# Feed-forward norm of a hybrid decoder: undivided halves of x written during attention's output product, the root applied to gate and up, new states one step at a time

## Chip, cores and metric

The kernel runs on one core of one Trainium2 chip (the chip is trn2). The metric is device time in microseconds of that core from start to end of one launch; three runs give a median. The engines are TensorE (PE in the profile, with PEld for its weight loads), VectorE (DVE), ScalarE (ACT), GpSimd (POOL) and SyncE (SP), whose queue starts the DMAs.

## What is computed

The reference is one inference step of two layers on 1024 prompt tokens and 8 x 4 sample tokens (1056 columns in all), model width 1024, feed-forward width 2816. Of a layer, cut to what matters here:

```python
    x = x + jnp.concatenate([o_attn, y_ssm], axis=-1) @ p['w_out']   # o_attn 512 wide, y_ssm 1024 wide
    hn = rms_norm(x, p['norm_ffn'])                                   # x * rsqrt(mean(x*x) + EPS) * g
    g, up = jnp.split(hn @ p['w_gate_up'], [D_FF], axis=-1)
    x = x + (jax.nn.silu(g) * up) @ p['w_down']
```

Besides x the layer returns window keys and values, the convolution's last rows, and the new recurrent state of every sample, `h * exp(sum) + sum_t B_t (x) xdt_t`, for 8 samples and 16 heads of 64 x 128. These sample states are the "new states" below.

## The kernel before

Everything lies transposed: x is eight tiles `big` of 128 rows (model width) by 1056 tokens. Tokens are taken in three column groups `t` of TW = 352. Products are made in three passes (`mm3`, lines 258 to 265): each float32 operand is divided into a rounded part and a remainder (`split`, line 226, for activations: ACT casts, DVE or POOL subtracts; `load_next`, line 237, for weights: ACT casts at line 243, POOL subtracts at line 244), and PE adds hi x hi, hi x lo and lo x hi into one PSUM bank. A product of eight 128-row blocks is 24 matmuls of 352 columns, one of four blocks is 12. These products use three rotating banks `g`; all else uses five banks `p`. So the result of a product has to be read out of its bank before the third product after it starts.

The order of work on each engine is in program order as far as dependencies allow, but the framework's scheduler weaves it; engines then run their queues strictly in order. `Flow` (line 81) holds side work as generators: every `tick` (one per product) steps the queue of side work once, runs what `later` put off by a number of ticks, and, for the `slow` queue, makes two steps placed behind the last instruction named as `anchor`.

The stages around the change, per layer:

- Attention (lines 1030 to 1098) is side work during `one_ssm` (line 1189), the output product of the state-space rows: product m is three 24-matmul groups. L1066 and L1067 are the score matmuls, L1017 the scores with mask on DVE, L1024 the exponential on ACT, L1027 the division on DVE, L1082 the transposes on PE (copied out at L1083), L1090 the products with v (copied out at L1093). Products m = 0 to 5 run with attention; then `flow.need` finishes attention, its result is split (L228, L232), product 6 follows.
- Attention's output product (loop from line 1210): eight m, three t, 12 matmuls each; m = 7 takes the state-space rows of m = 7 along. After each, DVE adds it to x (L1217), ACT squares (L318) and DVE adds up the squares in `acc` (L319).
- The norm (`norm_end`, line 321): four one-column matmuls sum the squares over the rows (L292), DVE takes the root by three Newton steps on 88 x 4 numbers (`rsqrt`, lines 275 to 281), PE spreads it over all rows (L300), and for each of eight blocks DVE multiplies x by gain and root (L325), ACT casts (L228), POOL or DVE subtracts (L232).
- The feed-forward block: `hpair` (line 1224) makes gate (part 0) and up (part 1) for 22 blocks f; ACT reads the gate from its bank with SiLU (L1234), DVE multiplies by up (L1236) and the result is split for the down product. The first f goes t by t, gate and up; the others gate for three t, then up. Blocks of 5, 5, 4, 4, 4 f are followed by `accumulate` (line 334), the down product, whose results DVE adds to x at L343.
- The new states (`new_states`, line 1240): 16 tiles, two buffers `F`; each is loaded with its B rows (L1245, L1246), gets four steps of one scaling (L1249) and four multiply-adds (L1251) on DVE, and is written back (L1253). They start 45 ticks into the feed-forward block, two steps a tick.

Of the kernel before, what the change touches and what calls it, by code (L numbers as in the profile page):

```python
# [10 lines left out]
F32 = mybir.dt.float32  # L11
# [6 lines left out]
P = 128  # L18
# [62 lines left out]
class Flow:  # L81


    def __init__(self, tc):
        self.tc, self.anchor = tc, None
        self.queue, self.slow, self.soon, self.open = deque(), deque(), [], set()

    def push(self, name, gen, after=0):
# [8 lines left out]

    def push_slow(self, name, gen):
        self.open.add(name)
        self.slow.append((name, gen))  # L100
# [12 lines left out]
    def tick(self, n=1):  # L113
        due = []
        for e in self.soon:
            e[0] -= 1
            if e[0] < 0:
                due.append(e)
        for e in due:
            self.soon.remove(e)  # L120
            e[1]()
        for _ in range(n + (len(self.queue) > 1)):
            self.step()
        if self.slow and self.anchor:

            with self.tc.issue_after(self.anchor.ins):
                for _ in range(2):
                    self.step(self.slow)
# [20 lines left out]
def body(ctx: ExitStack, tc, A, outs):  # L149
# [170 lines left out]

    def norm_end(x, gcol, u, t, acc):
        r = on_all(rstd_of(acc, D))
        for k in range(KD):
            s = mk("nu", [P, TW], bufs=3)
            V.scalar_tensor_tensor(s, x[k][:, tsl(t)], gcol(k), r, op0=ALU.mult, op1=ALU.mult)  # L325
            split(u[0][t][:, k, :], u[1][t][:, k, :], s, G if k % 4 else V)
# [10 lines left out]
    def accumulate(x, name, nk, xs, norm=None, after=None):  # L337
# [17 lines left out]
        if late:  # L355
            ws = [weights(name + (m,)) for m in (4, 6)]
            for t in range(NT):
                for m in range(4, 8):
                    one(m, t, ws[m // 2 - 2], m % 2 * P)
                if norm:  # L360
                    gcol, u, acc = norm
                    flow.later(lambda t=t: norm_end(x, gcol, u, t, acc[t]))
                else:
                    after(t)
# [10 lines left out]
    for l in range(L):  # L375
# [21 lines left out]
        for part in IN_ORDER:  # L397
# [5 lines left out]
            wlist.append(((l, part), a))  # L403
        for m in list(range(7)) + [("a", m) for m in range(7)] + [7, ("a", 7)]:
            if isinstance(m, int):
# [95 lines left out]
    for l in range(L):  # L501
# [699 lines left out]
        for t in range(NT):  # L1201
            for i in range(4):
                split(ohl[i][0][:, tsl(t)], ohl[i][1][:, tsl(t)], qT[i][:, tsl(t)])
        one_ssm(6, weights((l, "ssm", 6)))

        u = act_tiles()
        acc = accs()
        for m in range(8):
            ws = [weights((l, "ssm", 7))] if m == 7 else []
            ws.append(weights((l, "attn", m)))  # L1210
            for t in range(NT):
                pt = gbank()
                if m == 7:
                    mm3(pt[:, 0:TW], ws[0], 0, P, halves(mix)(t), 8, stop=False)
                mm3(pt[:, 0:TW], ws[-1], 0, P, rows(ohl)(t), 4, start=(m < 7))
                d = x[m][:, tsl(t)]
                flow.anchor = V.tensor_tensor(d, pt[:, 0:TW], d, op=ALU.add)  # L1217
                norm_sq(m, d, acc[t])
                if m == 7:
                    flow.later(lambda t=t, l=l: norm_end(x, lambda k: g_ffn(l, k), u, t, acc[t]), 0)  # L1220
                flow.tick()


        def hpair(f, hh, hl, swap):
# [4 lines left out]
            for part, t in order:  # L1229
                pt = gbank()  # L1230
                mm3(pt[:, 0:TW], ws[part], 0, P, halves(u)(t), KD)
                if part == 0:
                    sg[t] = mk("R", [P, 380], bufs=3)[:, 0:TW]
                    SC.activation(sg[t], pt[:, 0:TW], AF.Silu)  # L1234
                else:
# [44 lines left out]

        flow.later(lambda g=new_states(): flow.push_slow("st", g), after=45)
        flow.open.add("st")
# [47 lines left out]
```

## Time and profile before

| | us |
|---|---|
| three runs, median (lowest to highest) | 2939.91 (2937.18 to 2940.93) |
| the profiled execution | 2939.68 |
| its span, first to last instruction | 2937.9 |
| PE busy, share of the span | 2862.7, 97% |
| DVE, ACT, POOL busy | 1501.2, 1023.3, 998.3 |
| chain that ended last | PE 78%, DVE 12%, DMA 5%, ACT 3% |

Layer 0 takes about the first half of the span, with attention's end near 611 to 638 us, attention's output product to 692 us, then the feed-forward block; the same places of layer 1 lie near 2063, 2090 and 2144 us. A PE record lasts about 0.32 us while the next starts 0.16 us after it, so two overlap: busy time on PE hides losses, and the count of records in a window is what shows them. "PEclk" is the granted share of TensorE's full clock (1.00 is the upper of its two levels, 2.4 GHz; at 1.2 GHz it is half).

### The profile page before, as it was taken

Reading aid. Unit: us, or ns where it says so; the run is one execution under the profiler, and the core shown is the slowest. Engines: PE = TensorE matmul, PEld = TensorE weight load, DVE = VectorE, ACT = ScalarE, POOL = GpSimd, SP = SyncE. Lnnn points to the kernel's source line nnn. Section 1 sums busy time; section 2 is a strip of 40 time slices with the busy share of each in tenths; the row PEclk is TensorE's granted clock in tenths of the full one; section 3 lists DMA queues with packets and bytes.
Section 4 is the critical chain, followed back from the end, with each engine's and each line's share of the span. In section 5 each row is a group of like instructions: output and inputs, shape, how many; then the busy total and the mean of one; then the engine's idle time right before and its main releaser. Section 6 shows DMA issues by size and latency. Waiting matters only on the chain.

```text
span 2937.9 us, 46615 instructions
## 1 busy us (share of the span) xinstructions
PE 2862.7 (97%) x18580; PEld 2746.3 (93%) x18580; DVE 1501.2 (51%) x3689; ACT 1023.3 (35%) x2043; POOL 998.3 (34%) x880
## 2 busy tenths in 40 slices
PE   8999999999999999999989999999999999999999
PEld 6999999879999999999978999998899999999999
DVE  7977747666149411121488677567641683121212
ACT  5564437553211111111256635465431111111111
POOL 5343327434223322222143423355342232222221
PEclk9999999999999999999999999999999999999999
DMA  5231223011125211111222312230111342111112
GB/s 186 74 89 58 78 57 112 17 29 55 46 70 152 69 54 37 58 37 54 73 79 76 88 52 78 56 104 19 40 51 40 98 136 60 52 45 43 54 37 81
DMA packets 307808, 197.76 MB, mean 67 GB/s; under 512 B 27742, under 2 KB 287110, under 8 KB 307560
## 3 DMA queue, kind: packets, MB, share of 16 engines
q1 hardware_dynamic: 307560, 194.79, 22.4%
q8 instruction: 146, 2.39, 0.3%
q14 instruction: 70, 0.57, 0.1%
q10 hardware_dynamic: 32, 0.01, 0.0%
HBM read 171.49 MB, written 25.30 MB: 67 GB/s over the span
## 4 chain that ended last, share of the span: by engine, by line
PE 78%; DVE 12%; DMA 5%; ACT 3%; issue 1%; POOL 1%; SPq 0%; DVEq 0%; POOLq 0%; ACTq 0%
PE g L263 23%; PE g L265 22%; PE g L264 22%; DVE F L1251 2%; DVE big L612 2%; PE p L1090 1%; DMA F<-acd 1%; DVE F L681 1%; ACT nu L897 1%; DMA out_dram<-F 1%; PE p L708 1%; PE p L719 1%; PE p L1082 1%; PE p L692 1%; PE p L778 1%
## 5 line engine op out<-in xcount | busy, mean ns | idle before, releaser
L263 PE MATMUL g<-ahi,whi 128*128 128x352 f32 (+1 forms) x3792 | 1244.3, 329 | 11.4 <-DVE R L1236 6.9
L264 PE MATMUL g<-alo,whi 128*128 128x352 f32 (+1 forms) x3792 | 1230.9, 325 | 7.2 <-DVE alo L232 4.1
L265 PE MATMUL g<-ahi,w 128*128 128x352 f32 (+1 forms) x3792 | 1233.2, 325 | 0.0
L244 POOL TENSOR_TENSOR w<-w,whi 128x1024 fp32r<-128x1024 f32 (+3 forms) x250 | 514.9, 2060 | 1178.5 <-ACT whi L243 937.5
L263 PEld LDWEIGHTS g<-ahi,whi 128*128 128x128 f32 (+1 forms) x3792 | 715.2, 189 | 29.7 <-DVE R L1236 9.2
L264 PEld LDWEIGHTS g<-alo,whi 128*128 128x128 f32 (+1 forms) x3792 | 717.8, 189 | 15.7 <-DVE alo L232 5.5
L265 PEld LDWEIGHTS g<-ahi,w 128*128 128x128 f32 (+1 forms) x3792 | 716.4, 189 | 8.8 <-issue 6.1
L243 ACT CAST whi<-w 128x1024 fp32r<-128x1024 f32 (+3 forms) x250 | 226.1, 904 | 717.0 <-PE g L264 654.9
L1236 DVE TENSOR_TENSOR R<-R,g 128x352 f32<-128x352 f32 x132 | 68.6, 519 | 650.4 <-PE g L265 650.4
L263 PE MATMUL g<-A,whi 128*128 128x352 f32 x1104 | 356.4, 324 | 0.2
L265 PE MATMUL g<-A,w 128*128 128x352 f32 x1104 | 356.0, 322 | 0.0
L264 PE MATMUL g<-F,whi 128*128 128x352 f32 x960 | 310.9, 324 | 0.8 <-DVE F L232 0.6
L343 DVE TENSOR_TENSOR big<-g,big 128x352 f32<-128x352 f32 x240 | 125.7, 524 | 323.3 <-PE g L265 323.2
L263 PEld LDWEIGHTS g<-A,whi 128*128 128x128 f32 x1104 | 207.4, 188 | 0.8 <-DVE big L343 0.7
L265 PEld LDWEIGHTS g<-A,w 128*128 128x128 f32 x1104 | 207.3, 188 | 0.0
L264 PEld LDWEIGHTS g<-F,whi 128*128 128x128 f32 x960 | 180.4, 188 | 5.6 <-DVE F L232 2.4
L228 ACT CAST A<-R 128x352 fp32r<-128x352 f32 x132 | 64.2, 486 | 348.4 <-DVE R L1236 347.7
L1251 DVE SCALAR_TENSOR_TENSOR F<-F,xdds 128x128 f32<-128x128 f32 x512 | 164.2, 388 | 3.2 <-DMA F<-cbd 3.1
L612 DVE SCALAR_TENSOR_TENSOR big<-R,vc,big 128x352 f32<-128x352 f32 (+2 forms) x240 | 140.3, 609 | 15.4 <-ACT big L610 14.3
L685 POOL TENSOR_TENSOR F<-F,A 128x1024 f32<-128x1024 f32 x32 | 87.8, 2744 | 145.3 <-ACT F L684 128.1
L1234 ACT ACTIVATE R<-g 128x352 f32<-128x352 f32 x132 | 60.6, 462 | 207.7 <-PE g L265 207.7
L232 POOL TENSOR_TENSOR F<-R,A 128x352 fp32r<-128x352 f32 x54 | 58.7, 1087 | 143.6 <-ACT A L228 143.6
(332 smaller groups left out, 3337.0 us busy)
## 6 DMA issues: line engine op xcount, KB each, us to landing
w<-in_w_gate_up_dram SPq DMA_DIRECT2D x88, 512.0 KB
w<-in_w_in_dram SPq DMA_DIRECT2D x44, 512.0 KB
F<-acd SPq DMA_DIRECT2D x32, 512.0 KB
out_dram<-F SPq DMA_DIRECT2D x42, 256.0 KB
w<-in_w_down_dram SPq DMA_DIRECT2D x32, 320.0 KB
w<-in_w_down_dram SPq DMA_DIRECT2D x40, 256.0 KB
xd<-big SPq DMA_DIRECT2D x16, 528.0 KB
big<-xd SPq DMA_DIRECT2D x16, 528.0 KB
```

What stands on the lines that cost most here:

```text
L228: SC.copy(hi, src)
L243: SC.copy(hi, raw)
L244: G.tensor_tensor(lo, raw, hi.bitcast(F32), op=ALU.subtract)
L263: TE.matmul(out, lhsT=hi[:, k, c], rhs=xh, start=(start and k == 0), stop=False)
L264: TE.matmul(out, lhsT=hi[:, k, c], rhs=xl, start=False, stop=False)
L265: TE.matmul(out, lhsT=lo[:, k, c], rhs=xh, start=False, stop=(stop and k == nk - 1))
L343: flow.anchor = V.tensor_tensor(d, pt[:, 0:TW], d, op=ALU.add)
L612: flow.anchor = V.scalar_tensor_tensor(d, r(w), c_w(l, w, m), d, op0=ALU.mult, op1=ALU.add)
L685: G.tensor_tensor(bc, bc, ct[:, sl].unsqueeze(1).to_broadcast([P, 2, 512]), op=ALU.mult)
L1234: SC.activation(sg[t], pt[:, 0:TW], AF.Silu)
L1236: flow.anchor = V.tensor_tensor(sg[t], sg[t], pt[:, 0:TW], op=ALU.mult)
L1251: V.scalar_tensor_tensor(st[:, jj, :], bb[:, t, :], xdds[:, j, b * 4 + t:b * 4 + t + 1], st[:, jj, :], op0=ALU.mult, op1=ALU.add)
```

## The change

1. Product m = 7 of the state-space rows is made right after product 6, by itself; attention's product m = 7 is then 12 matmuls as the others.
2. During attention's output product, each new block of x is at once written as its two halves times the gain, without the root: ACT multiplies and rounds (hi), DVE multiplies and subtracts (lo). The squares are added up by POOL and not by DVE.
3. `norm_end`'s 24 multiplications, casts and subtractions are dropped for this norm. The root is taken after m = 7, spread over all rows when the first gate product of that t is done, and copied to `rinv` (ACT). Gate is multiplied by it before SiLU and after it (the second stands for up's root). That is DVE, ACT, DVE where ACT stood alone, for all 22 f.
4. For the norm between the layers the root is taken two ticks ahead of the rest of `norm_end`.
5. `push_slow` takes a pace; new states go one step a tick.

```diff
-                for _ in range(2):
+                for _ in range(self.pace):
                     self.step(self.slow)
...
-    def norm_end(x, gcol, u, t, acc):
-        r = on_all(rstd_of(acc, D))
+    def norm_end(x, gcol, u, t, root):
+        r = on_all(root)
...
-                    flow.later(lambda t=t: norm_end(x, gcol, u, t, acc[t]))
+
+                    def root(t=t):
+                        y = rstd_of(acc[t], D)
+                        flow.later(lambda: norm_end(x, gcol, u, t, y))
+                    flow.later(root)
...
-        for m in list(range(7)) + [("a", m) for m in range(7)] + [7, ("a", 7)]:
+        for m in list(range(8)) + [("a", m) for m in range(8)]:
...
-        one_ssm(6, weights((l, "ssm", 6)))
+        for m in (6, 7):
+            one_ssm(m, weights((l, "ssm", m)))
...
+        r01, r2 = mk("sc", [P, 2, TW]), mk("xs3", [P, TW])
+        rinv = [r01[:, 0], r01[:, 1], r2]
...
+        def root(t):
+            roots[t] = rstd_of(acc[t], D)
+
         for m in range(8):
-            ws = [weights((l, "ssm", 7))] if m == 7 else []
-            ws.append(weights((l, "attn", m)))
+            w = weights((l, "attn", m))
             for t in range(NT):
                 pt = gbank()
-                if m == 7:
-                    mm3(pt[:, 0:TW], ws[0], 0, P, halves(mix)(t), 8, stop=False)
-                mm3(pt[:, 0:TW], ws[-1], 0, P, rows(ohl)(t), 4, start=(m < 7))
+                mm3(pt[:, 0:TW], w, 0, P, rows(ohl)(t), 4)
                 d = x[m][:, tsl(t)]
                 flow.anchor = V.tensor_tensor(d, pt[:, 0:TW], d, op=ALU.add)
-                norm_sq(m, d, acc[t])
+                hi = u[0][t][:, m, :]
+                SC.activation(hi, d, AF.Copy, scale=g_ffn(l, m))
+                V.scalar_tensor_tensor(u[1][t][:, m, :], d, g_ffn(l, m), hi.bitcast(F32), op0=ALU.mult, op1=ALU.subtract)
+                if m == 0:
+                    SC.activation(acc[t], d, AF.Square)
+                else:
+                    sq = mk("nsq", [P, TW], bufs=2)
+                    SC.activation(sq, d, AF.Square)
+                    G.tensor_tensor(acc[t], acc[t], sq, op=ALU.add)
                 if m == 7:
-                    flow.later(lambda t=t, l=l: norm_end(x, lambda k: g_ffn(l, k), u, t, acc[t]), 0)
+                    flow.later(lambda t=t: root(t))
                 flow.tick()
...
                 if part == 0:
+                    if t in roots:
+                        SC.copy(rinv[t], on_all(roots.pop(t)))
                     sg[t] = mk("R", [P, 380], bufs=3)[:, 0:TW]
-                    SC.activation(sg[t], pt[:, 0:TW], AF.Silu)
+                    V.tensor_tensor(sg[t], pt[:, 0:TW], rinv[t], op=ALU.mult)
+                    SC.activation(sg[t], sg[t], AF.Silu)
+                    V.tensor_tensor(sg[t], sg[t], rinv[t], op=ALU.mult)
...
-        flow.later(lambda g=new_states(): flow.push_slow("st", g), after=45)
+        flow.later(lambda g=new_states(): flow.push_slow("st", g, 1), after=45)
```

Three places show how instructions move. In the rows `g` is a product's bank, `p` another bank, `ahi`/`alo` the halves of an activation, `whi`/`w` those of a weight; the line numbers of the change are those of its own file.

The first is PE at the end of attention in layer 0 (L1082/L1088 transpose the weights of attention, L1090/L1096 multiply by v, L1066/L1072 make scores). Before:

```order
L265 MATMUL g_6739<-ahi_4784,w_6269 128x352
L1082 MATMUL p_6465<-cst,F_813_6212 128x128 x4
L1082 MATMUL p_6471<-cst,F_813_6212 128x128 x4
L1082 MATMUL p_6478<-cst,F_818_6239 128x128 x4
L1082 MATMUL p_6484<-cst,F_818_6239 128x128 x4
L1090 MATMUL p_6515<-F_847_6464,A_562_4232 64x512
L1090 MATMUL p_6515<-F_850_6477,A_562_4232 64x512
L1066 MATMUL p_6527<-xs_671_5087,sc_6490 128x256
```

With the change:

```order
L267 MATMUL g_6738<-ahi_4784,w_6269 128x352
L1088 MATMUL p_6465<-cst,F_813_6212 128x128 x4
L265 MATMUL g_6771<-ahi_4782,whi_6682 128x352
L266 MATMUL g_6771<-alo_4785,whi_6682 128x352
L267 MATMUL g_6771<-ahi_4782,w_6683 128x352
...
L265 MATMUL g_6771<-ahi_4782,whi_6682 128x352
L1088 MATMUL p_6471<-cst,F_813_6212 128x128 x4
L266 MATMUL g_6771<-alo_4785,whi_6682 128x352
L267 MATMUL g_6771<-ahi_4782,w_6683 128x352
L1088 MATMUL p_6478<-cst,F_818_6239 128x128 x4
L1088 MATMUL p_6484<-cst,F_818_6239 128x128 x4
```

The 72 matmuls of the state-space product m = 7 now stand among attention's last transposes, scores and products, all of them ahead of the last eight products with v but one; before, nothing of another kind stood there until attention's own output product began.

The second is PE at the step from attention's output product to the first gate product (L292/L294 sum squares, L300/L302 spread the root). Before:

```order
L265 MATMUL g_7382<-A_885_6654,w_7177 128x352
L300 MATMUL p_7247<-cst,r4y_7233 128x88 x4
L292 MATMUL p_7325<-cst,R_6772 88x1 x4
L263 MATMUL g_7494<-ahi_6765,whi_7182 128x352
L263 MATMUL g_7521<-ahi_6765,whi_7484 128x352
L264 MATMUL g_7494<-alo_6768,whi_7182 128x352
```

With the change:

```order
L267 MATMUL g_7419<-ahi_6849,w_7305 128x352
L294 MATMUL p_7346<-cst,R_6855 88x1 x4
L294 MATMUL p_7385<-cst,R_6856 88x1 x4
L265 MATMUL g_7419<-ahi_6849,whi_7304 128x352
...
L265 MATMUL g_7502<-ahi_6850,whi_7304 128x352
L302 MATMUL p_7444<-cst,r4y_7352 128x88 x4
L294 MATMUL p_7454<-cst,R_6857 88x1 x4
L266 MATMUL g_7502<-alo_6853,whi_7304 128x352
```

The sums of squares of t = 0 and t = 1 stand behind the first 18 matmuls of gate (g_7419), and the first root is spread behind gate, up (g_7474) and the first two matmuls of the next gate; before, root and halves stood ahead of the first gate matmul.

The third is DVE between two blocks f while new states are made (L1249/L1275 and L1251/L1277 are a state's steps, L1236/L1262 multiplies by up). Before:

```order
L1236 TENSOR_TENSOR R_9308<-R_9308,g_9400 128x352
L1249 TENSOR_SCALAR F_1190_9429<-F_1190_9429,eends_519 128x128 x4
L1251 SCALAR_TENSOR_TENSOR F_1190_9429<-F_1190_9429,xdds_518 128x128 x3
L232 TENSOR_TENSOR F_1172_9192<-R_9308,A_1171_9191 128x352
L1251 SCALAR_TENSOR_TENSOR F_1190_9429<-F_1190_9429,xdds_518 128x128 x10
L1249 TENSOR_SCALAR F_1203_9521<-F_1203_9521,eends_519 128x128 x3
...
L1251 SCALAR_TENSOR_TENSOR F_1203_9521<-F_1203_9521,xdds_518 128x128 x16
L1236 TENSOR_TENSOR R_9481<-R_9481,g_9571 128x352
```

With the change:

```order
L1262 TENSOR_TENSOR R_9210<-R_9210,g_9285 128x352
L1275 TENSOR_SCALAR F_1166_9314<-F_1166_9314,eends_519 128x128 x4
L1277 SCALAR_TENSOR_TENSOR F_1166_9314<-F_1166_9314,xdds_518 128x128 x3
L234 TENSOR_TENSOR F_1149_9100<-R_9210,A_1148_9099 128x352
L1277 SCALAR_TENSOR_TENSOR F_1166_9314<-F_1166_9314,xdds_518 128x128 x7
L1258 TENSOR_TENSOR R_9361<-g_9336,sc_6858 128x352
L1277 SCALAR_TENSOR_TENSOR F_1166_9314<-F_1166_9314,xdds_518 128x128 x6
L1260 TENSOR_TENSOR R_9361<-R_9361,sc_6858 128x352
```

Before, 40 state instructions stand between one reading of a bank by DVE and the next, with the change 14; the reading is now that of gate (L1258), three products earlier than that of up.

## Rows read from the trace of the kernel before

**Rows 1.** The page, part 1: busy us, share, instructions of each engine.
```profile
PE 2862.7 (97%) x18580; PEld 2746.3 (93%) x18580; DVE 1501.2 (51%) x3689; ACT 1023.3 (35%) x2043; POOL 998.3 (34%) x880
```

**Rows 2.** PE by stretch: window, length, busy (records), PEclk, DMA share, GB/s.
```profile
611.10:625.80 14.70, 12.13 (x67) 0.88 0.12 36
625.80:638.40 12.60, 12.14 (x53) 1.00 0.00 1
638.40:692.60 54.20, 54.20 (x342) 1.00 0.18 52
692.60:730.00 37.40, 32.35 (x188) 0.91 0.19 54
730.00:800.00 70.00, 70.00 (x442) 1.00 0.19 55
840.00:1000.00 160.00, 156.97 (x971) 0.99 0.41 118
1100.00:1300.00 200.00, 200.00 (x1248) 1.00 0.15 43
2062.90:2077.20 14.30, 11.28 (x66) 1.00 0.07 19
...
2144.20:2182.00 37.80, 33.87 (x190) 0.86 0.18 54
2300.00:2460.00 160.00, 155.83 (x952) 0.99 0.41 116
```

**Rows 3.** PE's timeline near attention's end: start, us, instruction, count.
```profile
603.22 1.94 PE L1090 MATMUL p<-F,A 128*64 128x512 f32 x8
...
611.23 1.91 PE L1082 MATMUL p<-cst,F 128*128 128x128 f32 x16
```

**Rows 4.** PE by line, 611.1 to 625.8: busy us, mean ns, idle before and releasers.
```profile
L1090 PE MATMUL p<-F,A 128*64 128x512 f32 x13 | 5.2, 764 | 2.4 <-ACT F L1083 2.4
L1082 PE MATMUL p<-cst,F 128*128 128x128 f32 x36 | 4.6, 278 | 0.1
```

**Rows 5.** PE by line, 692.6 to 730: busy, mean ns, idle before and releasers.
```profile
L264 PE MATMUL g<-alo,whi 128*128 128x352 f32 x53 | 18.7, 356 | 2.6 <-POOL alo L232 1.8 <-DVE alo L232 0.8
...
L300 PE MATMUL p<-cst,r4y 88*128 88x88 f32 x12 | 1.5, 245 | 1.6 <-DVE r4y L281 1.6
```

**Rows 6.** The timeline of all engines in attention's output product.
```profile
650.25 0.52 DVE L1217 TENSOR_TENSOR big<-g,big 128x352 f32<-128x352 f32 x1
650.87 0.50 ACT L318 ACTIVATE nsq<-big 128x352 f32<-128x352 f32 x1 [1.09 <-DVE big L1217]
651.40 0.53 DVE L319 TENSOR_TENSOR R<-R,nsq 128x352 f32<-128x352 f32 x1 [0.62 <-ACT nsq L318]
...
651.84 0.52 DVE L1217 TENSOR_TENSOR big<-g,big 128x352 f32<-128x352 f32 x1
652.40 1.29 POOL L244 TENSOR_TENSOR w<-w,whi 128x512 fp32r<-128x512 f32 x1 [4.04 <-ACT whi L243]
...
652.98 1.10 DVE L319 TENSOR_TENSOR R<-R,nsq 128x352 f32<-128x352 f32 x1 [0.62 <-ACT nsq L318]
```

**Rows 7.** DVE by line, 640 to 692.
```profile
L319 DVE TENSOR_TENSOR R<-R,nsq 128x352 f32<-128x352 f32 x20 | 16.6, 831 | 12.2 <-ACT nsq L318 12.2
```

**Rows 8.** POOL by line, 640 to 692.
```profile
L244 POOL TENSOR_TENSOR w<-w,whi 128x512 fp32r<-128x512 f32 (+1 forms) x7 | 11.3, 1611 | 27.4 <-ACT whi L243 27.4
```

**Rows 9.** POOL by line and shape, whole span: an addition of 352 columns.
```profile
L801 POOL TENSOR_TENSOR A<-A,nu 128x352 f32<-128x352 f32 x24 | 24.0, 1002 | 27.6 <-ACT nu L800 27.6
```

**Rows 10.** ACT by line and shape, whole span: scaling by a column.
```profile
L936 ACT ACTIVATE A<-g,vc 128x352 f32<-128x352 f32 x24 | 13.3, 553 | 0.4
```

**Rows 11.** DVE by line, 840 to 1000, while new states are made.
```profile
L1251 DVE SCALAR_TENSOR_TENSOR F<-F,xdds 128x128 f32<-128x128 f32 x256 | 80.7, 381 | 0.7 <-DMA F<-cbd 0.6
...
L1236 DVE TENSOR_TENSOR R<-R,g 128x352 f32<-128x352 f32 x15 | 7.7, 514 | 16.5 <-PE g L265 16.5
```

**Rows 12.** PE's timeline while new states are made.
```profile
911.69 0.43 PE L263 MATMUL g<-ahi,whi 128*128 128x352 f32 x1 [2.02 <-DVE R L1236]
```

More of the change, by code (lines that the diff above doesn't have):

```diff
@@ L86, in __init__ @@
         self.queue, self.slow, self.soon, self.open = deque(), deque(), [], set()
+        self.pace = 2
     def push(self, name, gen, after=0):
@@ L96, in later, with push_slow @@
         self.soon.append([after, f])
-    def push_slow(self, name, gen):
+    def push_slow(self, name, gen, pace=2):
+        self.pace = pace
         self.open.add(name)
@@ L1203, in body @@
                 split(ohl[i][0][:, tsl(t)], ohl[i][1][:, tsl(t)], qT[i][:, tsl(t)])
-        one_ssm(6, weights((l, "ssm", 6)))
+        for m in (6, 7):
+            one_ssm(m, weights((l, "ssm", m)))
         u = act_tiles()
         acc = accs()
+        r01, r2 = mk("sc", [P, 2, TW]), mk("xs3", [P, TW])
+        rinv = [r01[:, 0], r01[:, 1], r2]
+        roots = {}
+        def root(t):
+            roots[t] = rstd_of(acc[t], D)
         for m in range(8):
-            ws = [weights((l, "ssm", 7))] if m == 7 else []
-            ws.append(weights((l, "attn", m)))
+            w = weights((l, "attn", m))
             for t in range(NT):
                 pt = gbank()
-                if m == 7:
-                    mm3(pt[:, 0:TW], ws[0], 0, P, halves(mix)(t), 8, stop=False)
-                mm3(pt[:, 0:TW], ws[-1], 0, P, rows(ohl)(t), 4, start=(m < 7))
+                mm3(pt[:, 0:TW], w, 0, P, rows(ohl)(t), 4)
                 d = x[m][:, tsl(t)]
                 flow.anchor = V.tensor_tensor(d, pt[:, 0:TW], d, op=ALU.add)
-                norm_sq(m, d, acc[t])
+                hi = u[0][t][:, m, :]
[7 more added lines that the diff above has]
+                    G.tensor_tensor(acc[t], acc[t], sq, op=ALU.add)
                 if m == 7:
-                    flow.later(lambda t=t, l=l: norm_end(x, lambda k: g_ffn(l, k), u, t, acc[t]), 0)
+                    flow.later(lambda t=t: root(t))
                 flow.tick()
```

## Prediction

> **What bounds the kernel now.** I read the page's engine shares first: PE is busy 97% of the span, DVE 51%, ACT 35%, POOL 34% [rows 1]. So the end is set by PE, and a gain can only come from stretches in which PE does less than it could. Busy time hides those, because records overlap; therefore I next read the windows with their counts of records. In the down products 1248 matmuls of 352 columns take 200 us, 0.160 us each; in gate and up 442 take 70 us, 0.158 us each [rows 2]. That pitch is what PE can do: 3.8 us for a product of 24 matmuls, 1.9 us for one of 12. Held against it, each layer has three places where PE falls behind, and one where it does not:
>
> - Attention's end, 611.1 to 638.4 us: few records, and the granted clock is 0.88 in the first part, 1.00 in the second [rows 2].
> - Attention's output product, 638.4 to 692.6 us: 342 x 0.158 = 54.0 of 54.2 us. Nothing is lost.
> - The norm up to the first gate products, 692.6 to 730 us: 188 records in 37.4 us, clock 0.91 [rows 2].
> - The new states, 840 to 1000 us: 971 records in 160 us where 998 would fit [rows 2].
>
> Then I read the groups by line for what ended PE's waits in each [rows 4, 5], and the timelines for who holds whom [rows 6, 12]. The profiled execution took 2939.68 us (2937.9 of span and 1.8 around it), 0.2 below the median of the runs, so the sum below is set against 2939.7.
>
> **A, attention's end.** PE's prices without waits: a transpose 1.91/16 = 0.12 us, a product with v 1.94/8 = 0.243 [rows 3]; scores of 256 columns by their columns, 0.158 x 256/352 = 0.115. The first part holds 36 transposes and 13 products with v [rows 4], 16 scores and 2 others: 4.3 + 3.2 + 1.8 + 0.3 = 9.6 us of work in 14.7, so 5.1 are lost, the lower clock's share among them; in layer 1, with 66 records in 14.3, 4.7. The second part (53 records: 13 transposes, 12 products with v, 28 of 352 columns) holds 1.6 + 2.9 + 4.4 = 8.9 in 12.6 us, so 3.7 are lost. PE waits there for attention's chain on ACT, as for the copies of transposes (L1083) [rows 4], with nothing else in its queue. The change lays the 72 matmuls of product m = 7, 72 x 0.158 = 11.4 us, among just these rows. That is more than is lost, but they stand ahead of the last products with v, so the last copies and the splits of attention's result keep their distance to PE. I take the first part's loss and a little of the second: **5.5 a layer, 11 in both**. Bounds: 3.0 a layer if only the idle time that the busy columns admit comes back (14.70 - 12.13 and 12.60 - 12.14 [rows 2]), 8.6 if all does.
>
> **N, from the norm to gate.** Of the 188 records 28 are small: 37.4 - 160 x 0.158 - 28 x 0.12 = 8.7 us lost; in layer 1 (190 records, 24 of them small, clock 0.86) 37.8 - 166 x 0.158 - 24 x 0.12 = 8.7. The waits are for the halves from POOL, DVE and ACT and for the root [rows 5]. After the change the halves exist already when gate begins, and the root is needed only when gate is read out of its bank. PE has three banks, so three products, 11.5 us, pass before that reading holds it. What may remain are the sums of squares of t = 1, which stand behind 18 gate matmuls (2.8 us) and need POOL's last addition (1.0 us [rows 9], behind an ACT square of 0.50 [rows 6]), and the spreading of the root (L302). Today the root costs PE 1.6 [rows 5]; I leave 1.2 a layer, bounds 0 and 3.5.
>
> **U, the new load in attention's output product.** Today DVE adds (0.52) and sums squares (0.53), ACT squares [rows 6]. Now a product runs DVE add 0.52, ACT hi 0.55 (scaling by a column [rows 10]), DVE lo 0.53, so with a hand-over of some 0.04 about 1.64 us, during which DVE's queue stands still for ACT, against 1.90 us of PE. Over 24 products that leaves 24 x 0.26 = 6.2 us, and two products in spare banks are another 3.8: 10.0 us of cushion. Against it stands what POOL does to DVE: a DVE addition that runs beside a POOL subtraction took 1.10 us in place of 0.53 and ended 0.39 after POOL's end [rows 6]; over the stage 20 additions took 16.6 us, 6.0 more than 20 x 0.53, with POOL busy for 11.3 [rows 7, 8]. The change gives POOL 21 additions of 1.0 [rows 9]: 32.3 us busy. In proportion DVE would be held 6.0 x 32.3/11.3 = 17.2 us, 7.2 beyond the cushion: that is the upper bound, the lower is 0, because POOL's addition is released by the square, which ACT makes after hi, at the time when lo already runs. I take 1.5 a layer.
>
> The Trainium skill (SBUF — State Buffer, "SBUF: two separate sides") states as a rule that a VectorE operation with two SBUF inputs and a GpSimd operation lock one port pair against each other for a whole instruction; the held addition agrees. Its page GPSIMD Engine Reference, "Engine selection", speaks against the change: elementwise additions belong on VectorE, GpSimd being about twice as slow; 1.00 beside 0.53 agrees. By that rule alone the first rival below would be the forecast.
>
> N and U together: 8.7 - 1.2 - 1.5 = **6.0 a layer, 12 in both**; bounds from 8.7 - 3.5 - 7.2 = -2.0 to 8.7 a layer.
>
> **S, the new states.** 160 - 971 x 0.1603 = 4.3 us are lost in layer 0, 160 - 952 x 0.1603 = 7.4 in layer 1: 11.7. A state instruction takes 0.381 us on DVE [rows 11]; two steps a tick are ten, 3.8 us, as long as a product, and DVE has 0.51 for reading up [rows 11] and the splits besides. So its queue runs late by up to 40 state instructions (15.4 us) between two readings, and PE waits for a bank, 2.02 us at 911.69 [rows 12]. One step a tick is 1.9 us; with gate's two multiplications (0.52 and 0.53) 3.0 of 3.8. In the next block's down products of 15 matmuls (2.4 us) DVE has 1.9 + 0.52: some 24 of them run late by 0.05, 1.2 us in all, which the banks hold. Before the reading of gate 14 state instructions, 5.4 us, stand ahead, against two products of cushion, 7.6. I leave 0.8 a layer: **gain 10**, bounds 0 and 11.7.
>
> **Edits at nothing.** 66 gates a layer get two DVE multiplications, 66 x 1.05 = 69 us of DVE each, spread over 66 gate ticks of 3.8 us; DVE has half its time free [rows 1], and the cover is the three banks: without them each gate would cost PE the read, 0.5. SiLU from SBUF and three copies are ACT's, with 65% free. The earlier root of the norm between the layers leaves PE's order as it was. On SP, ACT and POOL, the loads, casts and subtractions of m = 7's state-space weights move ahead of attention's weights; their number is the same, and PE takes them in that order too. The first state load of layer 1 goes out later but stands far ahead of its use.
>
> **Sum.** 11 + 12 + 10 = 33 of 2939.7: **2907 us**. All terms at the top, 17 + 17.4 + 11.7 = 46, give 2893.6; all at the bottom, 6 - 4 + 0 = 2, give 2938.
>
> **The rivals.** (1) *DVE and POOL do share in proportion*, so U costs 7.2 a layer, 11.4 more than I took: 2918. For it the lengthened additions [rows 6, 7]; against it the order of hi, lo and square. 0.20. The Trainium skill's lock (SBUF — State Buffer, "SBUF: two separate sides") is this mechanism. (2) *The wait for new states stays*: one step a tick stretches them over twice as many products, into the short down products, and readings queue behind them there; S gains nothing: 2917. For it, the 2.42 against 2.4; against, the cushion. 0.10. (3) *The fill gives nothing*, that is, the change does not do what it does on paper: attention's end is set by the chain on ACT and DVE, the 72 matmuls delay the products with v as much as they cover: 2918. Against it, PE waits there for short copies only [rows 4]. 0.06. (4) *Slower: each lo and each addition hold one another in turn.* A product's DVE chain is then 1.64 + 1.0 (a whole POOL addition) + 0.47 (the part of a weight subtraction) = 3.1 against 1.90 of PE: 24 x 1.2 = 29, less the 3.8 of the banks, 25 a layer, 23.5 more than I took: 2907 + 47 = 2954. It decides the sign from a chain of 2.8 us: 0.91 late a product, 24 x 0.91 - 3.8 = 18 a layer, 16.5 more than I took, in both layers the sum's 33. Against it: POOL would have to be released just ahead of each lo. 0.04. My forecast has 0.60.
>
> **How the numbers follow.** A measurement of this kernel tells about 0.2%, 5.9 us, from no change. The forecast and the first three rivals give 2907 to 2918 and lie below 2934; two of them together with a weak A (3.0 in place of 5.5) give some 2929 to 2935. So faster 0.89, within 0.2% 0.07, slower 0.04. The range begins at 2892, all at the top, and ends at 2929, which takes in two rivals at once; the slower case and the worst sums are left out.
>
> **What the profile after should show.** A: attention's end with 72 more records and no longer in proportion, clock near 1.00. U: 12 matmuls still every 1.90 us, lo at 0.53 to 0.8 in the mean; a mean over 1.2 with PE waiting for DVE's x would speak for rivals 1 or 4. N: the first 160 gate and up matmuls in some 26.5 us, waits for the root at L294 or L302 under 1.5. S: over 990 records in 160 us, no wait of 2 us for DVE's reading; DVE with over 100 us more busy time. I am wrong if attention's output product takes over 57 us, or if the waits in the states' stretch move to gate's reading.

## The result and the profile after

The changed kernel takes 2904.5 us (median of four runs, 2902.42 to 2910.45), the kernel before 2939.49 (four runs, 2937.18 to 2940.93): the ratio is 0.9883, with a 95% interval of 0.9872 to 0.9895, or some 35 us. The forecast was 2907 with a range from 2892 to 2929. The profiled execution took 2903.36, with a span of 2901.4, against 2939.68 and 2937.9.

The page of the changed kernel, its first part (busy us, share, instructions), against [rows 1]:

```profile
PE 2842.4 (98%) x18580; PEld 2737.2 (94%) x18580; DVE 1718.6 (59%) x3905; ACT 1031.5 (36%) x2049; POOL 980.9 (34%) x886
```

PE has the same number of matmuls and DVE 217 us more work, in a span that is 36.5 us shorter. PE by stretch, the columns as in [rows 2]:

```profile
612.00:624.00 12.00, 12.00 (x80) 1.00 0.08 22
624.00:636.00 12.00, 12.00 (x80) 1.00 0.01 1
636.00:645.00 9.00, 8.88 (x44) 1.00 0.10 29
...
660.00:675.00 15.00, 15.00 (x95) 1.00 0.24 69
...
829.00:989.00 160.00, 160.00 (x1006) 1.00 0.32 92
...
2285.00:2445.00 160.00, 160.00 (x1006) 1.00 0.34 101
```

Attention's end (612 to 645) is now dense at full clock; attention's output product still makes a matmul every 0.158 us (95 in 15); and the 160 us with new states hold 1006 matmuls where there were 971 and 952. PE's waits from 686 to 735 us (what waited for what: us, times, longest), where the kernel before had 5.0 us of them (4.2 stand in [rows 5]), and then the same place of layer 1, 2118 to 2170 us:

```profile
PE g L265 <- DVE big L1231: 0.3, 1, 0.3
```

```profile
PE g L265 <- DVE big L1231: 0.9, 1, 0.9
```

These are PE's first gate matmuls, which wait until DVE has read x's block out of the bank that they are to use.

To see where the time went I take four marks at which both kernels have done the same work, and ask how far the changed one is ahead there: the reading of the last product of m = 5 (L1194, now L1200), the start of the last matmul of attention's output product, the sixth multiplication by up (L1236, now L1262), and the last addition of the down product (L343, now L345).

| mark | layer 0: before, after, ahead | layer 1: before, after, ahead |
|---|---|---|
| m = 5 read | 593.43, 596.89, -3.5 | 2045.23, 2031.13, 14.1 |
| attention's output made | 692.52, 688.88, 3.6 | 2143.97, 2123.40, 20.6 |
| sixth up | 750.95, 739.01, 11.9 | 2202.40, 2174.10, 28.3 |
| last down | 1475.71, 1458.59, 17.1 | 2930.52, 2894.05, 36.5 |

The differences between the rows are the terms of the forecast. Attention's end and its output product (A and U): 7.1 and 6.5, in all 13.6. The norm to gate (N): 8.3 and 7.7, in all 16.0. The new states (S): 5.2 and 8.2, in all 13.4. Together 43.0; and the stretches up to m = 5, which the forecast did not mention, took 3.5 and 3.0 longer. 43.0 - 6.5 = 36.5, the whole difference of the spans. All this compares one profile of each kernel; what that is worth is told behind the table below.

### The profile page after: what moved, and what is told of

It reads as the page before. It is cut to its first block, busy times and chain, and to the rows that moved or that the text cites. A ratio compares the mean times of both kernels' runs of the same rounds, so it can differ in the third digit from the quotient of the medians.

```text
span 2901.4 us, 46904 instructions
## 1 busy us (share of the span) xinstructions
PE 2842.4 (98%) x18580; PEld 2737.2 (94%) x18580; DVE 1718.6 (59%) x3905; ACT 1031.5 (36%) x2049; POOL 980.9 (34%) x886
## 3 DMA queue, kind: packets, MB, share of 16 engines
q8 instruction: 146, 2.39, 0.3%
## 4 chain that ended last, share of the span: by engine, by line
PE 81%; DVE 10%; ACT 5%; DMA 2%; issue 1%; POOL 1%; SPq 0%; DVEq 0%; ACTq 0%; POOLq 0%
PE g L265 24%; PE g L267 23%; PE g L266 23%; DVE big L618 2%; ACT nu L903 2%; DVE F L687 2%; PE p L1096 1%; DMA F<-acd 1%; PE p L714 1%; DVE alo L1234 1%; PE p L1088 1%; PE p L698 1%; DVE F L692 1%; PE p L725 1%; PE p L784 1%
## 5 line engine op out<-in xcount | busy, mean ns | idle before, releaser
L345 DVE TENSOR_TENSOR big<-g,big 128x352 f32<-128x352 f32 x240 | 125.4, 522 | 233.6 <-PE g L267 232.9
L1277 DVE SCALAR_TENSOR_TENSOR F<-F,xdds 128x128 f32<-128x128 f32 x512 | 203.9, 424 | 9.6
L1262 DVE TENSOR_TENSOR R<-R,g 128x352 f32<-128x352 f32 x132 | 68.9, 522 | 216.7 <-PE g L267 215.9
L1259 ACT ACTIVATE R<-R 128x352 f32<-128x352 f32 x132 | 65.6, 497 | 297.6 <-DVE R L1258 297.4
L1258 DVE TENSOR_TENSOR R<-g,sc 128x352 f32<-128x352 f32 x88 | 45.9, 522 | 127.4 <-PE g L267 124.8
```

Source lines behind the costliest of these rows:

```text
L1259: SC.activation(sg[t], sg[t], AF.Silu)
L1262: flow.anchor = V.tensor_tensor(sg[t], sg[t], pt[:, 0:TW], op=ALU.mult)
L1277: V.scalar_tensor_tensor(st[:, jj, :], bb[:, t, :], xdds[:, j, b * 4 + t:b * 4 + t + 1], st[:, jj, :], op0=ALU.mult, op1=ALU.add)
```

## The experiments

All were measured beside runs of the kernel before on the same chip. The table splits each profiled execution by the same marks: by how much it is ahead of the kernel before's profiled execution (both layers added) in the stretches up to m = 5 ("front"), from there to the sixth up ("middle": A, U and N), and from there to the last down product ("states": S).

| kernel | median us (lowest to highest) | ratio, 95% interval | front | middle | states |
|---|---|---|---|---|---|
| the change | 2904.5 (2902.42 to 2910.45) | 0.9883 [0.9872, 0.9895] | -6.5 | 29.6 | 13.4 |
| order alone | 2940.14 (2932.02 to 2945.19) | 0.9999 [0.9988, 1.001] | -6.8 | 2.4 | 2.7 |
| norm alone | 2941.1 (2936.83 to 2945.88) | 0.9999 [0.9988, 1.0009] | -10.9 | 19.2 | -11.8 |
| pace alone | 2929.04 (2927.6 to 2933.16) | 0.9959 [0.9948, 0.9971] | -3.1 | 0.6 | 13.1 |
| pace two | 2929.4 (2924.68 to 2931.79) | 0.9962 [0.9947, 0.9976] | -11.7 | 31.1 | -11.2 |
| root late | 2905.15 (2894.65 to 2906.76) | 0.9869 [0.9853, 0.9885] | -7.9 | 30.7 | 13.4 |
| no sums | 2906.16 (2901.47 to 2907.57) | 0.9881 [0.9864, 0.9897] | -8.1 | 29.4 | 12.4 |
| sums on DVE | 2902.31 (2900.7 to 2903.96) | 0.9871 [0.9857, 0.9886] | -2.5 | 29.9 | 11.8 |
| gate bare | 2898.19 (2896.88 to 2900.79) | 0.9859 [0.9844, 0.9873] | -3.2 | 30.9 | 13.4 |
| square first | 2900.76 (2897.36 to 2905.46) | 0.9875 [0.9858, 0.9891] | -2.8 | 31.9 | 13.3 |
| later root | 2909.29 (2906.44 to 2910.26) | 0.9897 [0.9882, 0.9912] | -9.3 | 30.9 | 12.2 |
| the change again | 2900.73 (2899.81 to 2909.36) | 0.9868 [0.9849, 0.9887] | -12.7 | 30.6 | 12.7 |
| square first again | 2904.42 (2895.35 to 2908.19) | 0.9864 [0.9843, 0.9885] | -13.5 | 31.9 | 13.4 |

In the kernels that keep parts 1, 3 and 5, middle and states repeat within 3 us, while the front moves by 11 us. So a part's effect is read from its own stretch. Two cautions go with that. The kernel before has a single profile, which is the zero of every row: order alone has its code from the sixth up on, and is 2.7 us ahead of it in the states all the same (-0.2 in layer 0, 2.9 in layer 1), so a gain in one stretch is known to some 3 us. And the stretches do not add up to the medians: middle and states put order alone 5.1 us ahead and norm alone 7.4, while their medians show nothing, within some 3.5 us. All thirteen fronts are longer than the one of the kernel before, and in the profiles that is where the difference lies. What a part does to the time of a launch is therefore read from the medians.

**One part at a time.** Order alone is the kernel before with

```diff
-        one_ssm(6, weights((l, "ssm", 6)))
+        for m in (6, 7):
+            one_ssm(m, weights((l, "ssm", m)))
```

and the list of weights and attention's product m = 7 to match.

> Before, with part 1 alone (the state-space product m = 7 made right after product 6; norm and states as before). Theory of independent losses: attention's end gives back 5.5 to 7.7 us a layer, in all 11 to 15 below before. Rival, the long products were a cover: in the kernel before, the 36-matmul products of m = 7 gave the norm of t = 0 and t = 1 time (two times 24 matmuls, 7.6 us a layer) in which root and halves were made; with 12 matmuls each these show, so the gain at attention's end is given back at the first gate: within 4 us of before, with attention's end free of waits in the trace and the wait at the first gate products 5 to 8 us longer than before in each layer.

The rival was right: the ratio is 0.9999. By the marks above, attention's end did give its time back, 7.1 and 6.8 us, as much as in the whole change (7.1 and 6.5). But from there to the sixth up this kernel lost 5.8 and 5.7, within the rival's 5 to 8, so that 1.3 and 1.0 were left. PE's waits of this kernel from 686 to 735 us:

```profile
PE p L300 <- DVE r4y L281: 6.4, 2, 5.9
PE g L263 <- ACT R L1232: 1.1, 1, 1.1
PE p L292 <- DVE R L319: 0.8, 1, 0.8
PE g L263 <- ACT ahi L228: 0.8, 2, 0.6
PE g L263 <- DVE R L1234: 0.3, 1, 0.3
```

The wait for the root was 1.6 us [rows 5] and is 6.4, in layer 1 too: the long products of m = 7 had been its cover. All waits together grew from 5.0 to 9.4 us; the rest of the 5.8 goes with a lower granted clock there (0.86 from 689.6 to 727 us, where [rows 2] had 0.91). Part 1 alone moves a hole from one side of attention's output product to the other.

Pace alone is the kernel before with

```diff
...
-        flow.later(lambda g=new_states(): flow.push_slow("st", g), after=45)
+        flow.later(lambda g=new_states(): flow.push_slow("st", g, 1), after=45)
```

> Before, with part 5 alone (new states one step a tick). My theory: the stretch of new states alone gives 10 to 14 us, the same as in the changed kernel, since no gate work on DVE is needed for it: 2925 to 2930. Rival, the gain belongs to the reading of the bank by gate on DVE three products earlier and not to the pace: 0 to 3 us. No wait of 2 us for the multiplication by up should be left by the first.

My theory held: 13.1 us in the states' stretch with the old gate, no wait of PE left from 820 to 1010 us or in the same place of layer 1, and a ratio of 0.9959. The kernel before waited there, from 820 to 1010 us, for the multiplication by up:

```profile
PE g L263 <- DVE R L1236: 2.9, 2, 2.0
```

Norm alone is the changed kernel with parts 1 and 5 undone, and so with parts 2 to 4:

```diff
-        for m in (6, 7):
-            one_ssm(m, weights((l, "ssm", m)))
+        one_ssm(6, weights((l, "ssm", 6)))
...
-        flow.later(lambda g=new_states(): flow.push_slow("st", g, 1), after=45)
+        flow.later(lambda g=new_states(): flow.push_slow("st", g), after=45)
```

> The changed kernel with parts 1 and 5 undone: m = 7 merged as before, new states two steps a tick, but halves without the root, sums on POOL, root at gate. My theory: the norm's 7.9 us a layer come back, and the states' stretch loses what it lost before or more, since gate adds 1.05 us to DVE a product: 2920 to 2930. If the states' stretch loses 5 us a layer more than before for the new gate work, the result is 2932 to 2940 and parts 3 and 5 belong together.

The second case: 19.2 us came back in the middle, 9.6 and 9.5 a layer, all of them between the end of attention's output product and the sixth up, and 7.5 and 4.3 were lost with the states. That leaves 7.4, but this profile's front is 10.9 longer, and in the medians nothing is left (0.9999). PE's waits of this kernel from 820 to 1010 us:

```profile
PE g L265 <- DVE R L1260: 7.6, 8, 1.5
PE g L265 <- DVE R L1264: 1.5, 1, 1.5
```

L1260 there is gate's reading out of its bank (L1258 of the change). The wait has moved from up to gate, as the forecast's last sentence feared, but because of the pace, not of the change as a whole.

Pace two, the changed kernel with part 5 undone, turns it round:

```diff
-        flow.later(lambda g=new_states(): flow.push_slow("st", g, 1), after=45)
+        flow.later(lambda g=new_states(): flow.push_slow("st", g), after=45)
```

> The changed kernel with part 5 alone undone (new states two steps a tick, with gate's multiplications on DVE in place). If the new gate work makes the states' stretch dearer than it was before, as the run with the norm parts alone suggests (it lost 7.5 and 4.3 us there beyond the kernel before), this loses the 14 us that the slower pace gave and some 12 more: 2928 to 2932, with PE waiting 8 to 10 us a layer for gate's reading on DVE. If the states' stretch costs what it cost before, it is 2918.

As the first case said: 2929.4, with 7.4 and 3.8 us lost in the states' stretch where the change gains 5.2 and 8.2, and PE waiting for gate's reading (the columns as above, 820 to 1010 us):

```profile
PE g L265 <- DVE R L1258: 7.4, 8, 1.5
PE g L265 <- DVE R L1262: 1.6, 1, 1.6
```

So part 5 is worth 13 us before the norm is changed and 13.4 + 11.2 = 24.6 after it. This run also prices part 1 beside the changed norm, since norm alone differs from it by part 1 only: 31.1 - 19.2 = 11.9 us in the middle, against 2.4 when it stands alone.

Root late undoes part 4:

```diff
-                    def root(t=t):
-                        y = rstd_of(acc[t], D)
-                        flow.later(lambda: norm_end(x, gcol, u, t, y))
-                    flow.later(root)
+                    flow.later(lambda t=t: norm_end(x, gcol, u, t, rstd_of(acc[t], D)))
```

> The changed kernel with part 4 undone (between the layers the root is taken with the rest of norm_end). My theory: no difference, within 2 us of the changed kernel's 2904.5. Rival: part 4 is what made layer 1's stretch up to attention 3 us longer than before; then this is 2 to 4 us faster than the changed kernel, 2901, and layer 1 from its last down product to its first state-space product takes 470 us in place of 471.7.

No difference, and layer 1's front stays 3.5 us longer than before; part 4 is not its cause.

**POOL against DVE in attention's output product.** No sums leaves out the additions for m = 1 to 7 (the sum of squares then holds m = 0 alone):

```diff
                     SC.activation(sq, d, AF.Square)
-                    G.tensor_tensor(acc[t], acc[t], sq, op=ALU.add)
```

Sums on DVE gives them back to DVE:

```diff
-                    G.tensor_tensor(acc[t], acc[t], sq, op=ALU.add)
+                    V.tensor_tensor(acc[t], acc[t], sq, op=ALU.add)
```

> The changed kernel without POOL's additions of squares for m = 1 to 7: the sums are left out, the squares are still made. Theory A, the additions hold nothing (each is released when lo already runs) and only POOL's weight subtractions hold lo: lo keeps its mean of 0.88 us and the time stays within 4 us of 2904.5. Theory B, DVE and POOL share in proportion (my first rival): of the 8 us that lo is longer than 0.53 each, two thirds go, lo falls to 0.65 us in the mean, and the wait for x at the first gate products (0.3 and 0.9 us) vanishes; the time can fall by no more than those 1.2 us.

> The changed kernel with the squares summed by DVE as before, and not by POOL. DVE then has 0.52 + 0.53 + 0.53 us of work a product, with the sum of one product placed between the addition and lo of the next, where DVE otherwise waits for ACT. Theory A: it fits into 1.90 us but for the products in which a weight subtraction holds DVE (7 a layer, by up to 1.9 us): 0 to 4 us a layer slower, 2904 to 2912. Theory B, the choice of POOL was what made the new load fit: 24 products x 0.3 late - 3.8 of cushion and the holding of some 8 us: 7 to 11 us a layer slower, 2918 to 2926.

Both times and the length of lo fit theory A. DVE by line from 645 to 692 us: first the changed kernel, then without the sums, then with the sums on DVE.

```profile
L1234 DVE SCALAR_TENSOR_TENSOR alo<-big,vc,ahi 128x352 fp32r<-128x352 f32 x23 | 20.2, 882 | 13.6 <-ACT ahi L1233 13.6
```

```profile
L1234 DVE SCALAR_TENSOR_TENSOR alo<-big,vc,ahi 128x352 fp32r<-128x352 f32 x23 | 19.7, 859 | 12.4 <-ACT ahi L1233 12.4
```

```profile
L1234 DVE SCALAR_TENSOR_TENSOR alo<-big,vc,ahi 128x352 fp32r<-128x352 f32 x23 | 20.4, 890 | 6.3 <-ACT ahi L1233 6.3
L1231 DVE TENSOR_TENSOR big<-g,big 128x352 f32<-128x352 f32 x24 | 12.4, 515 | 0.8 <-PE g L267 0.8
L1240 DVE TENSOR_TENSOR R<-R,nsq 128x352 f32<-128x352 f32 x19 | 9.8, 513 | 0.0
```

In this window lo nearly keeps its mean without POOL's additions, 0.859 us in place of 0.882; over all 24 of a layer it is 0.85 and 0.83 in place of 0.94 in both, still far from theory B's 0.65. The changed kernel's trace shows it directly: none of the 42 additions runs when a lo starts, so they hold no lo. The small rest may come about by way of the subtractions, which queue behind the additions on POOL; that was not tried apart. The wait for x at the first gate did go without the sums, as theory B said, but PE waits 1.0 us for the root there instead (L302), in both layers. On DVE the sums go where DVE waited for hi (13.6 us of idle time become 6.3), at 0.513 us each. What holds lo is the weight subtraction, seven times a layer (1.28 to 2.40 us; once another subtraction of POOL's, 0.84), as the changed kernel's timeline shows, first DVE, then POOL (start, us, instruction, idle before):

```profile
677.77 0.59 DVE L1234 SCALAR_TENSOR_TENSOR alo<-big,vc,ahi 128x352 fp32r<-128x352 f32 x1 [0.66 <-ACT ahi L1233]
678.27 0.52 DVE L1231 TENSOR_TENSOR big<-g,big 128x352 f32<-128x352 f32 x1
679.58 2.39 DVE L1234 SCALAR_TENSOR_TENSOR alo<-big,vc,ahi 128x352 fp32r<-128x352 f32 x1 [0.79 <-ACT ahi L1233]
```

```profile
678.20 0.96 POOL L1240 TENSOR_TENSOR R<-R,nsq 128x352 f32<-128x352 f32 x1 [0.72 <-ACT nsq L1239]
679.20 2.40 POOL L246 TENSOR_TENSOR w<-w,whi 128x1024 fp32r<-128x1024 f32 x1
681.55 1.23 POOL L1240 TENSOR_TENSOR R<-R,nsq 128x352 f32<-128x352 f32 x1
```

POOL's addition starts at 678.20, 0.16 us before lo ends, and neither is longer for it; the addition of x beside it, which reads a bank, takes its 0.52. The subtraction starts 0.38 us ahead of the next lo, which then ends 0.37 us after it. DVE holds POOL as well: the addition at 681.55 starts with 0.42 us of that lo left and takes 1.23 us, as do 14 of the 42 additions, where the others take 0.96.

Square first exchanges the order on ACT, so that POOL is let go earlier:

```diff
-                hi = u[0][t][:, m, :]
-                SC.activation(hi, d, AF.Copy, scale=g_ffn(l, m))
-                V.scalar_tensor_tensor(u[1][t][:, m, :], d, g_ffn(l, m), hi.bitcast(F32), op0=ALU.mult, op1=ALU.subtract)
...
                     G.tensor_tensor(acc[t], acc[t], sq, op=ALU.add)
+                SC.activation(hi, d, AF.Copy, scale=g_ffn(l, m))
+                V.scalar_tensor_tensor(u[1][t][:, m, :], d, g_ffn(l, m), hi.bitcast(F32), op0=ALU.mult, op1=ALU.subtract)
```

> The changed kernel with ACT's square placed ahead of hi, so that POOL's addition is released some 0.5 us before lo and runs when lo wants to start: the mechanism of my slower rival, made on purpose. If POOL's additions hold lo whenever they start before it, lo lasts 1.0 to 1.4 us in the mean in place of 0.88, the chain of a product passes 1.90 us and PE waits for x at the end of attention's output product: 3 to 12 us a layer slower than the changed kernel, 2910 to 2928. If holding by additions of this kind does not exist, lo stays below 0.9 us and the time within 4 us of 2904.5.

The holding is there, the loss is not. In this kernel an addition of POOL runs when lo starts in 14 and 15 of the 24 products of a layer, and it does lengthen lo (0.89 in place of 0.58; DVE, then POOL):

```profile
659.59 0.89 DVE L1240 SCALAR_TENSOR_TENSOR alo<-big,vc,ahi 128x352 fp32r<-128x352 f32 x1 [0.53 <-ACT ahi L1239]
660.40 0.51 DVE L1231 TENSOR_TENSOR big<-g,big 128x352 f32<-128x352 f32 x1
661.81 0.53 DVE L1231 TENSOR_TENSOR big<-g,big 128x352 f32<-128x352 f32 x1 [0.89 <-PE g L267]
```

```profile
659.16 0.94 POOL L1238 TENSOR_TENSOR R<-R,nsq 128x352 f32<-128x352 f32 x1 [0.48 <-ACT nsq L1237]
```

But lo lasts 0.94 and 0.96 us in the mean of a layer, as in the changed kernel (0.94): neither the 1.0 to 1.4 that I expected of holding nor the less than 0.9 without it. And here the scheduler put two additions of x ahead of two lo, so DVE waits less for ACT and more for PE, and PE waits for nothing from 640 to 735 us. My expectation priced the holding and not what the scheduler would do with the new order; the middle is even 1.3 to 2.3 us shorter than in the change's two profiles. So it does not show what the slower rival would cost in an unchanged order; that was not tried.

**The gate.** Gate bare leaves out the root at gate for f = 1 to 21, with SiLU reading the bank as before:

```diff
-                    V.tensor_tensor(sg[t], pt[:, 0:TW], rinv[t], op=ALU.mult)
-                    SC.activation(sg[t], sg[t], AF.Silu)
-                    V.tensor_tensor(sg[t], sg[t], rinv[t], op=ALU.mult)
+                    if f == 0:
...
+                    else:
+                        SC.activation(sg[t], pt[:, 0:TW], AF.Silu)
```

> The changed kernel without the root at gate for f = 1 to 21: gate goes from its bank through SiLU on ACT as before, and the two multiplications by the root are left out. My forecast costed them at nothing, hidden by three banks: the time stays within 4 us of 2904.5, and the stretch of gate, up and down products has the same length within 0.5 us a layer. Rival: DVE's second multiplication, held by POOL's weight subtractions (2.3 us in place of 0.52 for every third), delays readings somewhere: 3 to 8 us faster.

By its stretches the forecast's zero holds: from the sixth up to the last down product it gains 5.2 and 8.2 us, as the change does. The median is 6 us lower, which the rival could claim. Of the 4.6 us by which its profiled execution is shorter, 3.3 lie in the front, where both kernels have the same code, and 1.3 in the middle, which is within what the middle varies; the medians by themselves do not exclude the rival.

**Two attempts at something better.** Later root adds two yields before the state-space norm's root is spread.

```diff
             yield
             yield
+            yield
+            yield
             for h in range(2):
```

> An attempt to beat both kernels: the changed kernel with the root of the state-space norm spread over the rows four ticks after it is begun and not two (two more yields in gnorm). In the changed kernel PE waits 4.4 us (layer 0) and 5.1 us (layer 1) for this root. If this is waiting for a late chain on DVE only, two more products of 24 matmuls cover it: 7 to 9 us faster, 2896 to 2898, and no wait over 1 us at that line. If the chain itself moves later with it, or the scaling of y behind it becomes late, 0 to 3 us.

A miss: PE still waits 4.0 and 5.3 us there, and the time is no better. Why the chain on DVE moved along with it was not followed up.

> The changed kernel as it is, beside the next one on the same chip. Two questions. First, its stretches before attention took 3.5 us (layer 0) and 3.0 us (layer 1) longer than in the kernel before, though the order of instructions in layer 0's is the same: if that varies from one execution to another, this profile shows other lengths there by 2 us or more, and from the state-space products to gate the same 14 to 16 us a layer below before; if it belongs to the change, it shows 3.5 and 3.0 again. Second, what the next kernel is compared with: 2902 to 2908.

> The kernel with the square ahead of hi once more, beside the changed one. If its 2900.8 was a better order (from the state-space products to gate it took 0.7 to 1.6 us a layer less than the changed kernel), it is 1 to 3 us below the changed kernel here; if it was the stretches before attention that happened to be short, both agree within 2 us and by the intervals cannot be told apart.

The changed kernel's second profile fell on its slowest run, 2909.36. Its front lost 4.8 and 7.9 us, the middle gained 15.6 and 15.0. So the front varies by several us between executions of the same code. The two orders of ACT agree as far as these runs can tell (intervals 0.9849 to 0.9887 and 0.9843 to 0.9885). No version here is shown to beat the change.

## Why the prediction was right

- **A and U, attention's output.** Forecast 5.5 - 1.5 = 4.0 a layer, measured 7.1 and 6.5. A is the whole of it: order alone, without the new load, gains 7.1 and 6.8, norm alone, with the old order, 0.0. It lies inside its bounds of 3.0 to 8.6; I had given too little to the second part, which is dense as well. U was over-sized: what it costs is PE's wait for x at the first gate, 0.3 and 0.9 us, behind a lo that a weight subtraction holds (by the marks it falls in N). The additions hold nothing, for the reason given there: POOL's addition is released when lo already runs. But lo's mean, 0.94, lies above the 0.53 to 0.8 that I named, by the subtractions alone; the cushion took it.
- **N.** Forecast 8.7 - 1.2, measured 8.3 and 7.7; without the 0.3 and 0.9 for x it is 8.6 in both. The cushion of three banks held: nothing waits for the root or the sums, so the residual of 1.2 was 0. The 26.5 us that I named for the first 160 gate and up matmuls are 28.8, because I had left out the 36 small ones that now stand among them.
- **S.** Forecast 3.5 and 6.6 (4.3 and 7.4 less 0.8), measured 5.2 and 8.2. Nothing of the loss was left, so the residual was 0. The rest is the pitch: I took 998 matmuls to fit into 160 us, and the changed kernel has 1006, so the losses that I read were 35 x 0.159 = 5.6 and 54 x 0.159 = 8.6 us. Against order alone's profile in place of the kernel before's, the same stretch gains 5.4 and 5.2.
- **What the forecast lacked.** The front cost 6.5 us in the pair of profiles. PE and DVE have the same order of instructions up to there in layer 0 of both kernels (on ACT and POOL one weight tile, at 571 us, is another), and 3.1 us are behind by 311 us already. That stretch was between 2.8 us shorter and 8.1 longer in the other runs, and in the change's own two profiles 3.5 and 4.8 longer. The waits that differ most there are PE's for the state-space scan on DVE. But in every profile of the table the front, both layers added, is longer than in the one profile of the kernel before, and that execution as a whole was no quick one (2939.68 against medians of 2939.49 and, of 23 runs beside order alone, 2940.24). So either its front was quick and the rest slow, or something in all the variants makes the front longer; this stays open. The sum came out right by 2.5 us because terms that were 10 us too small met a stretch that it did not have: that is luck.
- **The step that held only in company.** I added the terms as if each stood alone. By the medians the two gains of the forecast that are not the pace are worth nothing by themselves: order alone 0, norm alone 0, pace alone 11 us, all three 35. By middle and states it is 5.1, 7.4 and 13.7, against 43.0 together. The sum was right because all the parts were in it: N removes what order alone lays bare (the root behind m = 7), which makes part 1 worth 11.9 us in the middle in place of 2.4, and S takes away the queue in which gate's reading would stand. "Edits at nothing" was right for the change as it is, and wrong at the old pace, where that same gate work costs 24.6 - 13.1 = 11.5 us.
- **The rivals.** The first (proportional sharing) fell with no sums: what counts is which of the two instructions starts first, and not POOL's busy time. The second fell with the dense windows, the third with those and with order alone's 7.1 us. The fourth was not met; square first brought its holding about, but not in the order that it was priced for.

The Trainium skill's rule (SBUF — State Buffer, "SBUF: two separate sides"), that one of the two engines takes the shared ports for a whole instruction, agrees with 2.39 beside 2.40 us. Its rule on which engine should add (GPSIMD Engine Reference, "Engine selection") is right for the instruction, 0.513 against 0.96, and made no difference to this kernel that the runs could tell: 0.9871 with the sums on DVE.

## What to carry to other kernels

Before a long stretch of matmuls is moved to fill a hole, ask what it covers where it stands now: its removal may open a hole of the same size. Parts of a change that share an engine or a cover are priced together, and each is tested alone and left out, since the two prices can differ by the whole gain. When executions differ by several us somewhere else, compare marks at equal work and not only medians.

## Not expected of the hardware

Gate's second multiplication has both operands in SBUF. For one t in three it ran into the subtraction of the next weights on POOL: all 44 start while one runs and take 1.11 to 2.50 us, and none of the other 88 takes more than 0.53. DVE by line and shape, whole span of the changed kernel, and then one such case (DVE, POOL):

```profile
L1260 DVE TENSOR_TENSOR R<-R,xs 128x352 f32<-128x352 f32 x44 | 94.9, 2157 | 31.3 <-ACT R L1259 31.3
L1260 DVE TENSOR_TENSOR R<-R,sc 128x352 f32<-128x352 f32 x88 | 46.2, 524 | 46.2 <-ACT R L1259 46.2
```

```profile
773.57 0.53 DVE L1258 TENSOR_TENSOR R<-g,xs 128x352 f32<-128x352 f32 x1 [2.15 <-PE g L267]
774.89 2.48 DVE L1260 TENSOR_TENSOR R<-R,xs 128x352 f32<-128x352 f32 x1 [0.79 <-ACT R L1259]
```

```profile
774.59 2.40 POOL L246 TENSOR_TENSOR w<-w,whi 128x1024 fp32r<-128x1024 f32 x1 [9.12 <-ACT whi L245]
```

The same operation takes 2.157 us for the third t and 0.524 for the other two: 44 x 1.63 = 72 us of DVE that the forecast (69 us a layer for both multiplications) did not have. It cost nothing, as gate bare shows, at one step a tick. Whether it is these long multiplications that make gate's reading late at two steps a tick was not tried apart.
